# FFN inputs as 384 and 384 columns over two PSUM banks, gate with up in the last FFN, 64-row score products of two maps side by side

## The chip, the core and the metric

The kernel runs on one core of a Trainium2 chip. Its time is the time of one execution on the device in microseconds, the median of several runs. TensorE (PE in the rows) multiplies matrices and writes into PSUM; PEld is its weight load, which runs beside the matmuls. VectorE (DVE), ScalarE (ACT) and GpSimd (POOL) work on what it leaves. SyncE (SP) issues most transfers.

## The reference

Two layers over 512 latent tokens and 256 context tokens, 1024 channels wide, all in fp32. Each layer is a half FFN, a token mixer, and a second half FFN; each part is preceded by an RMS norm with shift and scale from a conditioning vector, and followed by another norm, a gate and the residual add. Layer 0 mixes by differential attention, layer 1 by a gated scan in both directions (HGRN2). In layer 1 the context tokens end with the mixer, so that the last FFN has only the 512 latent tokens.

```
def swiglu(h, w_in, w_out):
    gate, up = jnp.split(h @ w_in, 2, axis=-1)
    return (jax.nn.silu(gate) * up) @ w_out

# differential attention: 8 heads, two maps of 64 channels each
s = jnp.einsum('bqhmd,bkhmd->bhmqk', q, k) * scale
p = softmax(s)
a = p[:, :, 0] - lam * p[:, :, 1]

# HGRN2: q, two forget gates, input, output gate are projections of h
f = lb + (1 - lb) * sigmoid(f_logit)
```

The inner width of an FFN is 2816, so 22 chunks of 128 columns for the gate and 22 for the up part.

## The kernel before

Every fp32 operand of a large product is split in two: a high part (a cast on ScalarE) and a low part (the subtraction on VectorE), both of type fp32r. A product is then three passes, named in PASSES: high by high, high by low, low by high. `split` (lines 187 and 188) makes the two parts.

The order of all instructions is written by hand: each engine carries its instructions out in the order in which the program names them. The tile pools only add the waits: a new tile in a pool whose buffers are all in use waits until the last reader of an older tile is done.

**FFN.** `ffn` goes through the 22 chunks in groups, of which the first has one chunk and the seven others have three. For each chunk the gate is projected into a PSUM tile `pg`, the up part into `pu`, both from the pool ps_mm, which has two buffers of two banks (1024 columns) each. `proj` runs over the 8 slices of the contraction and the three passes, first for the 512 latent columns (24 matmuls into the first bank), then, where there is context, for the 256 context columns (24 matmuls into the second bank). ScalarE takes the silu of `pg`, VectorE multiplies it with `pu`, and the product is split into the tile `a`. After a group is complete, its output tiles (`out_tile`, line 653, 6 or 4 of them, each 18 matmuls of 512 columns which go to the two banks of a ps_mm tile in turn) are issued behind the gate of the next group's first chunk; VectorE adds each to `y` (line 670).

**Weights.** The class `Jobs` holds the list of all weight transfers and conversions in their order: gate, up and output weight of chunk 0, then of chunk 1, and so on. A transfer lands in one of three `raw` buffers, and is split into one of three `hl` buffers (gate and up) or three `wo` buffers. `need(key, ahead)` issues the conversions up to the one asked for and then up to `ahead` further gate or up weights; it stops at an output weight whose group is not open yet:

```
while self.done < n and self.gates.get(self.done, True) in self.open:
```

A group is opened by `J.open.add((l, i, c0))`, which stands behind the issue of the output tiles.

**Attention.** Heads are handled in four pairs; a generator `attn` is stepped by `T` between the matmuls of the next pair's projections (in the last pair: between those of the attention's output projection). An item is one head and 128 queries. For each of its two maps, `scores_softmax` multiplies a stacked operand of 128 rows (512 and 256 key columns) and then adds the missing product of 64 rows, with rows 0 to 63 for map 0 and 64 to 127 for map 1 (lines 954 and 955). VectorE takes the maximum of a map (line 957), then come the transposes of the item before, then the exponentials. The context queries have only the 256 context columns.

**HGRN.** For each of the 8 heads four projections of 128 channels go into tiles of the pool ps_tp (three buffers of one bank each): the two forget gates for all 768 columns, q and the output gate for 512. The sigmoids are lines 1388 (512 columns) and 1391 (256). Between the projections' matmuls `T` steps the scan of the head before.

## Time and profile before

| what | value |
|---|---|
| time, median of 3 runs | 3145.73 us (3143.97 to 3150.5) |
| the profiled execution's own time | 3149.13 us |
| its span, first to last instruction | 3147.3 us |
| TensorE busy | 3046.8 us, 97% |
| VectorE, ScalarE busy | 1716.1 and 961.3 us |
| mean granted TensorE clock | 0.985 |

The profile is that of one execution. Its span is 1.8 us shorter than that execution's time, and that time is 3.4 us above the median. A matmul's duration in the rows holds its way through the array, which overlaps with the next one; how fast matmuls follow each other is read from the starts, or from the length of a row that merges many.

### The profile page before, as it was taken

The numbers are of one execution on the slowest core, as the hardware profiler recorded it, in microseconds if no ns is written. First come the engines' busy times: TensorE is split into PE (matmuls) and PEld (weight loads), VectorE is DVE, ScalarE is ACT, GpSimd is POOL, SyncE is SP. The second block draws the span as 40 slices with busy tenths as digits, with TensorE's granted clock in tenths as the row PEclk, the third lists the DMA queues.
The fourth block names the chain that finished last, engine by engine and source line by source line (L and its number), as shares of the span: only waits on it lengthen the run. The fifth ranks groups of instructions, "written<-read, shape, count | busy, mean of one in ns | idle before, by whom it ended". The sixth has DMA issues, their size and how long they took to land.

```text
span 3147.3 us, 41132 instructions
## 1 busy us (share of the span) xinstructions
PE 3046.8 (97%) x17122; PEld 2577.1 (82%) x17122; DVE 1716.1 (55%) x2393; ACT 961.3 (31%) x1597; POOL 185.8 (6%) x235
## 2 busy tenths in 40 slices
PE   7999999989999899999999999999999999899998
PEld 5888888878877678888888888888889988678887
DVE  4555555646655674444446554444656565754344
ACT  4111111534444351111115111111444343442222
POOL 0000000131211020000001000000100000000000
PEclk9999999999988999999999999999999999999999
DMA  5333333254334233333222333333211111423231
GB/s 223 108 121 115 121 113 114 102 131 129 79 106 121 94 111 103 100 101 100 94 87 68 108 107 122 115 119 114 100 61 61 52 50 41 144 97 101 81 112 62
DMA packets 109546, 321.77 MB, mean 102 GB/s; under 512 B 11728, under 2 KB 12208, under 8 KB 109360
## 3 DMA queue, kind: packets, MB, share of 16 engines
q1 hardware_dynamic: 104432, 301.26, 30.4%
q0 software_dynamic: 3200, 11.59, 1.1%
q10 hardware_dynamic: 1728, 6.29, 0.5%
q8 instruction: 135, 2.21, 0.3%
q14 instruction: 51, 0.42, 0.0%
HBM read 292.83 MB, written 26.26 MB: 101 GB/s over the span
## 4 chain that ended last, share of the span: by engine, by line
PE 84%; DVE 4%; ACT 4%; issue 3%; DMA 2%; POOL 1%; SPq 0%; ACTq 0%; DVEq 0%; POOLq 0%
PE mm L574 43%; PE mm L653 21%; PE tp L574 8%; PE tp L1375 2%; PE mm L954 1%; PE gv L1012 1%; PE tp L653 1%; PE tp L1151 1%; PE mm L1285 1%; PE mm L955 1%; ACT tmp L395 1%; PE tp L992 1%; ACT tmp L545 1%; DMA mw<-in_w_mod_dram 1%; DVE hl L188 1%
## 5 line engine op out<-in xcount | busy, mean ns | idle before, releaser
L574 PE MATMUL mm<-hT,hl 128*128 128x256 f32 (+1 forms) x7728 | 1409.0, 342 | 8.1 <-DVE hT L550 3.3
L574 PEld LDWEIGHTS mm<-hT,hl 128*128 128x128 f32 x7728 | 1200.9, 188 | 208.1 <-DVE hT L550 6.7
L653 PE MATMUL mm<-wo,a 128*128 128x512 f32 x2886 | 664.9, 390 | 0.5 <-DVE wo L188 0.5
L653 PEld LDWEIGHTS mm<-wo,a 128*128 128x128 f32 x2886 | 538.5, 188 | 115.4 <-DVE y L668 2.6
L670 DVE TENSOR_TENSOR y<-y,mm 128x1024 f32<-128x1024 f32 x163 | 199.0, 1221 | 500.3 <-PE mm L653 500.3
L574 PE MATMUL tp<-hT,hl 128*128 128x512 f32 (+1 forms) x1824 | 381.4, 359 | 7.2 <-DVE aT L999 5.0
L188 DVE TENSOR_TENSOR hl<-raw,hl 128x1024 fp32r<-128x1024 f32 x250 | 304.6, 1229 | 149.8 <-ACT hl L187 149.8
L574 PEld LDWEIGHTS tp<-hT,hl 128*128 128x128 f32 x1824 | 291.4, 191 | 52.6 <-DVE aT L999 6.6
L292 DVE SCALAR_TENSOR_TENSOR acc<-mw,cs,acc 128x512 f32<-128x512 f32 x392 | 271.5, 745 | 2.8 <-DMA mw<-in_w_mod_dram 1.3
L187 ACT CAST a<-tmp 128x768 fp32r<-128x768 f32 (+1 forms) x88 | 68.8, 781 | 664.1 <-DVE tmp L747 664.1
L187 ACT CAST hl<-raw 128x1024 fp32r<-128x1024 f32 x250 | 258.2, 1046 | 25.3 <-DMA raw<-in_w_in_dram 20.6
L187 ACT CAST wo<-raw 128x1024 fp32r<-128x1024 f32 x94 | 98.0, 1044 | 464.0 <-PE mm L653 457.6
L731 ACT ACTIVATE tmp<-mm 128x768 f32<-128x768 f32 (+1 forms) x88 | 66.8, 759 | 405.4 <-PE mm L574 404.2
L747 DVE TENSOR_TENSOR tmp<-tmp,mm 128x768 f32<-128x768 f32 (+1 forms) x88 | 77.9, 886 | 200.8 <-PE mm L574 198.8
L188 DVE TENSOR_TENSOR a<-tmp,a 128x768 fp32r<-128x768 f32 (+1 forms) x88 | 78.5, 892 | 74.6 <-ACT a L187 74.6
L188 DVE TENSOR_TENSOR wo<-raw,wo 128x1024 fp32r<-128x1024 f32 x94 | 114.7, 1222 | 6.8 <-ACT wo L187 6.8
L653 PE MATMUL tp<-hl,hT 128*128 128x512 f32 x300 | 89.5, 432 | 16.5 <-DVE hl L188 5.1
L957 DVE TENSOR_REDUCE nm<-mm 128x1 f32<-128x768 f32 (+1 forms) x96 | 73.4, 776 | 54.8 <-PE mm L955 51.9
L653 PEld LDWEIGHTS tp<-hl,hT 128*128 128x128 f32 x300 | 55.7, 201 | 31.8 <-DVE aT L999 7.5
L964 ACT ACTIVATE pt<-mm,nm 128x768 f32<-128x768 f32 (+1 forms) x96 | 72.6, 767 | 29.5 <-DVE nm L957 29.4
L994 ACT CAST aT<-tp 128x384 fp32r<-128x384 f32 (+1 forms) x80 | 33.7, 461 | 144.5 <-PE tp L992 144.4
L1151 PE MATMUL tp<-hl,hT 128*128 128x256 f32 x576 | 75.1, 284 | 0.1
(189 smaller groups left out, 2439.0 us busy)
## 6 DMA issues: line engine op xcount, KB each, us to landing
raw<-in_w_in_dram SPq DMA_DIRECT2D x176, 512.0 KB, 4.5
mw<-in_w_mod_dram SPq DMA_DIRECT2D x144, 512.0 KB, 4.4
raw<-in_w_out_dram SPq DMA_DIRECT2D x88, 512.0 KB, 3.4
raw<-in_hg_w_dram SPq DMA_DIRECT2D x32, 512.0 KB, 3.3
raw<-in_da_qk_dram SPq DMA_DIRECT2D x16, 512.0 KB, 3.7
gg<-gg_d POOLq DMA_DIRECT2D x12, 512.0 KB, 4.6
xp<-x_d SPq DMA_DIRECT2D x10, 512.0 KB, 8.0
raw<-in_da_v_dram SPq DMA_DIRECT2D x8, 512.0 KB, 3.4
```

The costliest lines, as they stand in the source:

```text
L187: nc.scalar.copy(out=dst_hi, in_=src)
L188: nc.vector.tensor_tensor(out=dst_lo, in0=src, in1=dst_hi.bitcast(F32), op=ALU.subtract)
L292: nc.vector.scalar_tensor_tensor(out=acc[:, m], in0=raw[:, kk], scalar=cs[:, k, m:m + 1], in1=acc[:, m], op0=ALU.mult, op1=ALU.add)
L574: nc.tensor.matmul(out=ps_ap, lhsT=w[a], rhs=mv[b], start=(k == 0 and i == 0), stop=(k == nk - 1 and i == 2))
L653: nc.tensor.matmul(out=po if small else po[:, hh * 512:(hh + 1) * 512], lhsT=aT[ci][:, u, t * P:(t + 1) * P], rhs=wos[ci][:, v, hh * 512:( ...
L670: nc.vector.tensor_tensor(out=dst, in0=dst, in1=src, op=ALU.add)
L731: nc.scalar.activation(out=sg[:, :width], in_=pg[:, :width], func=AF.Silu)
L747: nc.vector.tensor_tensor(out=sg[:, :width], in0=sg[:, :width], in1=pu[:, :width], op=ALU.mult)
L957: nc.vector.tensor_reduce(out=nm, in_=sc[:, :n], axis=AX.X, op=ALU.max, negate=True)
L964: nc.scalar.activation(out=pt[:, :n], in_=scs[m][:, :n], func=AF.Exp, bias=nms[m], accum_out=s0s[hh][:, t:t + 1] if m == 0 else s1)
L1151: nc.tensor.matmul(out=pv[:, tt], lhsT=hT[:, k, a, t * P:(t + 1) * P], rhs=wk[:, b], start=(k == 0 and i_ == 0), stop=(k == KC - 1 and i_ ...
L1375: nc.tensor.matmul(out=pv[:, tt], lhsT=hT[:, k, a, t * P:(t + 1) * P], rhs=wk[:, b], start=(k == 0 and i_ == 0), stop=(k == KC - 1 and i_ ...
```

## The change

There are three edits.

1. A new helper `proj_banks` issues for each slice and pass one matmul for each of its blocks, each block with its own PSUM bank. In the three FFNs over 768 columns a projection now has two blocks of 384 columns, with the same weights, in the two banks of its ps_mm tile (`halves`); silu and multiplication read the two halves through a view (`flat`). The two forget gates of HGRN are done in the same way, in two ps_tp tiles, and each has two sigmoids of 384 columns.
2. In the last FFN (512 columns), from chunk 1 on, gate and up are issued together: one block each, the gate in the first bank of a single ps_mm tile and up in the second. Both calls of `need` stand in front of it, and so before `J.open.add`. The silu and the multiplication stay where they were.
3. In `scores_softmax` the 128-row products of both maps come first; then the 64-row products, for each block of key columns map 0 and map 1 one after the other. The two maximum reductions follow behind all of them.

```diff
--- before.py
+++ after.py
@@ -575,6 +575,16 @@
                 out=ps_ap, lhsT=w[a], rhs=mv[b],
                 start=(k == 0 and i == 0), stop=(k == nk - 1 and i == 2))
 
+    def proj_banks(blocks, tick=None):
+
+        for k in range(KC):
+            for i, (u, v) in enumerate(PASSES):
+                for w, ps, hT, a, b in blocks:
+                    nc.tensor.matmul(out=ps, lhsT=w[:, u, k], rhs=hT[:, k, v, a:b],
+                                     start=(k == 0 and i == 0), stop=(k == KC - 1 and i == 2))
+            if tick:
+                tick(3 * sum(e[4] - e[3] for e in blocks) / 2400.0)
+
     def proj(w, hT, pt, a, b, tick=None):
 
         for k in range(KC):
@@ -678,6 +688,15 @@
         pend = None
         hT = None
         slots = 2 * FC - 5
+
+        def halves(ap):
+
+            return ap.rearrange("p (b c) -> p b c", b=2)[:, :, 0:NTOK // 2]
+
+        def flat(ap, like):
+
+            return ap[:, :width].rearrange("p (b c) -> p b c", b=2) if len(like.shape) == 3 else ap[:, :width]
+
         J.open.add((l, i, 0))
         for gi, (c0, gn) in enumerate(GROUPS):
             aT = []
@@ -685,6 +704,8 @@
             for c in range(c0, c0 + gn):
                 pg = ps_mm([P, D])
                 pu = None
+                both = nt == LT and c != 0
+                pgv = pg[:, :width] if c == 0 or both else halves(pg)
                 if c == 0:
                     pu = ps_mm([P, D])
                     wg = J.need(("w", l, i, c, 0))
@@ -723,28 +744,33 @@
                     wg = J.need(("w", l, i, c, 0), 2)
                     M.pace(slots)
                     slots -= 1
-                    proj(wg, hT, pg[:, 0:NLAT], 0, NLAT)
-                    if nt == NT:
-                        proj(wg, hT, pg[:, NLAT:NTOK], NLAT, NTOK)
+                    if both:
+                        wu = J.need(("w", l, i, c, 1), 2)
+                        M.pace(slots)
+                        slots -= 1
+                        puv = pg[:, NLAT:2 * NLAT]
+                        proj_banks(((wg, pgv, hT, 0, NLAT), (wu, puv, hT, 0, NLAT)))
+                    else:
+                        proj_banks([(wg, pgv[:, b], hT, 384 * b, 384 * b + 384) for b in range(2)])
                 M.due()
                 sg = tmp([P, D])
-                nc.scalar.activation(out=sg[:, :width], in_=pg[:, :width], func=AF.Silu)
+                nc.scalar.activation(out=flat(sg, pgv), in_=pgv, func=AF.Silu)
                 if pend is not None:
                     aT_, wos_, first_ = pend
                     pend = None
                     for t in range(nt):
                         out_tile(t, aT_, wos_, y, first_)
                 J.open.add((l, i, c0))
-                if c != 0:
-                    pu = ps_mm([P, D])
+                if c == 0:
+                    puv = pu[:, :width]
+                elif not both:
+                    puv = halves(ps_mm([P, D]))
                     wu = J.need(("w", l, i, c, 1), 2)
                     M.pace(slots)
                     slots -= 1
-                    proj(wu, hT, pu[:, 0:NLAT], 0, NLAT)
-                    if nt == NT:
-                        proj(wu, hT, pu[:, NLAT:NTOK], NLAT, NTOK)
+                    proj_banks([(wu, puv[:, b], hT, 384 * b, 384 * b + 384) for b in range(2)])
                 M.due()
-                nc.vector.tensor_tensor(out=sg[:, :width], in0=sg[:, :width], in1=pu[:, :width], op=ALU.mult)
+                nc.vector.tensor_tensor(out=flat(sg, puv), in0=flat(sg, puv), in1=puv, op=ALU.mult)
                 a = fp.tile([P, 2, NTOK], F32R, tag="a", name="a", bufs=3)
                 split(a[:, 0, :width], a[:, 1, :width], sg[:, :width])
                 if c == FC - 2:
@@ -943,20 +969,23 @@
                 if t == 0:
                     s0s[hh] = sm.tile([P, NT], F32, tag="s0", name="s0", bufs=3)
                 s1 = sm.tile([P, 1], F32, tag="s1", name="s1")
-                nms, scs = [], []
+                nms = []
+                scs = [ps_mm([P, D]) for _ in range(2)]
+                cols = ([(slice(0, NLAT), slice(0, NLAT))] if t < LT else []) + [(slice(n - NCTX, n), slice(NLAT, NTOK))]
                 for m in range(2):
-                    sc = ps_mm([P, D])
-                    r0 = 64 * m
-                    for i in range(2):
-                        lhs = st_[:, m, t * P:(t + 1) * P] if i == 0 else st_[r0:r0 + 64, m, t * P:(t + 1) * P]
-                        rhs = st_[:, 2 + m] if i == 0 else st_[r0:r0 + 64, 4]
-                        if t < LT:
-                            nc.tensor.matmul(out=sc[:, 0:NLAT], lhsT=lhs, rhs=rhs[:, 0:NLAT], start=(i == 0), stop=(i == 1))
-                        nc.tensor.matmul(out=sc[:, n - NCTX:n], lhsT=lhs, rhs=rhs[:, NLAT:NTOK], start=(i == 0), stop=(i == 1))
+                    for o, i in cols:
+                        nc.tensor.matmul(out=scs[m][:, o], lhsT=st_[:, m, t * P:(t + 1) * P], rhs=st_[:, 2 + m, i],
+                                         start=True, stop=False)
+
+                for o, i in cols:
+                    for m in range(2):
+                        r = slice(64 * m, 64 * m + 64)
+                        nc.tensor.matmul(out=scs[m][:, o], lhsT=st_[r, m, t * P:(t + 1) * P], rhs=st_[r, 4, i],
+                                         start=False, stop=True)
+                for m in range(2):
                     nm = sm.tile([P, 1], F32, tag="nm", name="nm")
-                    nc.vector.tensor_reduce(out=nm, in_=sc[:, :n], axis=AX.X, op=ALU.max, negate=True)
+                    nc.vector.tensor_reduce(out=nm, in_=scs[m][:, :n], axis=AX.X, op=ALU.max, negate=True)
                     nms.append(nm)
-                    scs.append(sc)
                 lo = between()
                 pts = []
                 for m in range(2):
@@ -1383,17 +1412,18 @@
             for kd_ in range(4):
                 u = J.need(("hw", h, kd_), 2)
                 pl = ps_tp([P, 512])
-                proj(u, hT, pl, 0, NLAT, T)
                 if kd_ < 2:
-                    nc.scalar.activation(out=F[:, kd_, 0:NLAT], in_=pl, func=AF.Sigmoid)
-                    pc = ps_tp([P, 256])
-                    proj(u, hT, pc, NLAT, NTOK, T)
-                    nc.scalar.activation(out=F[:, kd_, NLAT:], in_=pc, func=AF.Sigmoid)
+
+                    pc = ps_tp([P, 512])
+                    proj_banks(((u, pl[:, 0:384], hT, 0, 384), (u, pc[:, 0:384], hT, 384, NTOK)), T)
+                    nc.scalar.activation(out=F[:, kd_, 0:384], in_=pl[:, 0:384], func=AF.Sigmoid)
+                    nc.scalar.activation(out=F[:, kd_, 384:], in_=pc[:, 0:384], func=AF.Sigmoid)
                     nc.vector.tensor_scalar(out=F[:, kd_], in0=F[:, kd_], scalar1=oml[:, kd_, h:h + 1],
                                             scalar2=lbv[:, kd_, h:h + 1], op0=ALU.mult, op1=ALU.add)
                     nc.vector.tensor_scalar(out=Kt[:, kd_], in0=F[:, kd_], scalar1=-1.0, scalar2=1.0,
                                             op0=ALU.mult, op1=ALU.add)
                 else:
+                    proj(u, hT, pl, 0, NLAT, T)
                     dst = qv if kd_ == 2 else gs
                     nc.scalar.activation(out=dst, in_=pl, func=AF.Sigmoid)
                     nc.vector.tensor_tensor(out=dst, in0=dst, in1=pl, op=ALU.mult)
```

## Rows read from the trace of the kernel before

**Rows 1.** The page: busy engines, and the chain by engine and line.
```profile
PE 3046.8 (97%) x17122; PEld 2577.1 (82%) x17122; DVE 1716.1 (55%) x2393; ACT 961.3 (31%) x1597; POOL 185.8 (6%) x235
...
PE 84%; DVE 4%; ACT 4%; issue 3%; DMA 2%; POOL 1%; SPq 0%; ACTq 0%; DVEq 0%; POOLq 0%
```

**Rows 2.** Stretches: length, busy PE PEld DVE ACT POOL (x count), PEclk, DMA share, GB/s.
```profile
640.00:990.00 350.00, 327.74 (x2005) 275.00 (x2004) 203.25 (x341) 148.11 (x332) 71.64 (x54) 0.95 0.45 117
...
2788.00:3122.00 334.00, 334.00 (x1443) 270.07 (x1442) 132.75 (x129) 82.97 (x101) 0.00 (x0) 1.00 0.29 92
```

**Rows 3.** Chain in order of time, first and last FFN: start, us, what.
```profile
359.59 24.50 PE mm L653 x108
384.09 8.40 PE mm L574 x48
...
2827.59 16.35 PE mm L653 x72
2843.93 33.60 PE mm L574 x144
```

**Rows 4.** Timeline of TensorE: attention-value product; last output tile.
```profile
762.60 2.31 PE L1012 MATMUL gv<-aT,vh 128*128 128x256 f32 x18
...
3134.64 4.24 PE L653 MATMUL tp<-wo,a 128*128 128x512 f32 x18
```

**Rows 5.** Timeline at a joint of two groups in the last FFN.
```profile
2842.20 1.99 ACT L187 CAST hl<-raw 128x1024 fp32r<-128x1024 f32 x2
...
2843.77 33.76 PE L574 MATMUL mm<-hT,hl 128*128 128x512 f32 x144
2843.97 1.22 DVE L670 TENSOR_TENSOR y<-y,mm 128x1024 f32<-128x1024 f32 x1 [2.87 <-PE mm L653]
2845.11 1.22 DVE L188 TENSOR_TENSOR wo<-raw,wo 128x1024 fp32r<-128x1024 f32 x1
...
2849.57 0.69 DVE L747 TENSOR_TENSOR tmp<-tmp,mm 128x512 f32<-128x512 f32 x1 [0.97 <-PE mm L574]
2850.29 0.62 ACT L187 CAST a<-tmp 128x512 fp32r<-128x512 f32 x1 [6.10 <-DVE tmp L747]
2850.82 1.04 ACT L187 CAST wo<-raw 128x1024 fp32r<-128x1024 f32 x1
...
2851.89 1.23 DVE L188 TENSOR_TENSOR wo<-raw,wo 128x1024 fp32r<-128x1024 f32 x1 [0.26 <-ACT wo L187]
```

**Rows 6.** Timeline of the first FFN's first output tiles.
```profile
70.14 2.59 DVE L668 COPY y<-mm 128x1024 f32<-128x1024 f32 x2 [3.56 <-PE mm L653]
...
71.42 2.59 PEld L653 LDWEIGHTS mm<-wo,a 128*128 128x128 f32 x12 [0.38 <-DVE y L668]
```

**Rows 7.** Busy time by stretch around two waits of TensorE, columns as in rows 2.
```profile
2755.00:2758.50 3.50, 0.00 (x0) 0.00 (x0) 2.63 (x3) 1.63 (x5) 2.41 (x4) 1.00 0.00 0
2758.50:2765.30 6.80, 5.82 (x24) 5.21 (x25) 3.96 (x7) 6.75 (x12) 2.60 (x4) 0.50 0.00 0
...
2461.50:2465.00 3.50, 3.50 (x19) 3.50 (x18) 1.98 (x3) 0.00 (x0) 0.24 (x1) 0.51 0.00 0
```

**Rows 8.** Timeline of one item's score products.
```profile
736.20 0.39 PE L954 MATMUL mm<-stk 128*128 128x512 f32 x1
...
736.43 0.28 PE L955 MATMUL mm<-stk 128*128 128x256 f32 x1
736.63 0.18 PEld L954 LDWEIGHTS mm<-stk 64*128 64x128 f32 x1 [0.24 <-issue]
...
736.97 0.28 PE L955 MATMUL mm<-stk 64*128 64x256 f32 x1
...
738.27 0.88 PE L992 MATMUL tp<-ident,pt 128*128 128x128 f32 x6
```

**Rows 9.** Timeline of TensorE: products with 32 output rows.
```profile
1199.01 0.64 PE L315 MATMUL gv<-acc,pick 128*32 128x128 f32 x16
```

**Rows 10.** The sigmoid of line 1388: ns min/median/max, first and last start, form.
```profile
L1388 ACT ACTIVATE F<-tp x16: 588/592/606, 2289.7 to 2651.6; 128x512 f32<-128x512 f32 x16
```

## The prediction

> **What bounds the kernel now.** I read the page's busy shares and its chain first [rows 1]. TensorE is busy 97% of the span and holds 84% of the chain; what is to be seen is that no other engine comes near, so a saving counts if it shortens the row of matmuls, and a loss counts if TensorE has to stand still. The stretches [rows 2] say where it stands: in the last FFN (2788 to 3122 us) it is busy 334.00 of 334.00 us, in the attention stretch 327.7 of 350. So the last FFN has no idle time that could soak up a new wait. The paces come from the chain in order of time [rows 3]: 48 matmuls of an FFN input (24 of 512 columns, 24 of 256) take 8.40 us; 144 of 512 columns in the last FFN take 33.60, so 233.3 ns each; 108 matmuls of the FFN output take 24.50, so 226.9 each. The 256-column ones are therefore (8.40 - 24 x 0.2333) / 24 = 116.7 ns. A pair of 512 and 256 costs 350 ns now.
>
> **Part 1, 384 and 384 columns over two banks.** The instruction count stays; 126 projections in the three long FFNs and 16 in HGRN, 24 pairs each, make 3408 pairs. No row has 384 columns. At 2.4 GHz 384 columns are 160 ns; the rows give what lies on top. On the same operands it is 10 ns at 256 columns and 20 ns at 512; the straight line gives 15, so 175 per matmul and 350 per pair: no change. The tempting reading is that the output's 227 comes from its two banks in turn. The trace speaks against that: the very last tile writes 9 matmuls in a row into one bank, and 18 of them take 4.24 us, of which the last one's own 0.39 comes off, so 3.85 / 17 = 226 ns [rows 4]. The attention-value product, also one bank, 256 columns, takes (2.31 - 0.28) / 17 = 119 ns, again some 13 on top. So 13 ns on top goes with other operands, not with alternation. If the pairs did get 13 ns: 346.7, or -3.3 x 3408 = -11 us. The ends: 10 on top gives 340 per pair, -34 us; 20 on top gives 360, +34 us. I take -3, next to the straight line on the same operands. In the last FFN 1008 matmuls could gain 6.4 ns each by the same argument (-6 us); I count nothing.
>
> **Part 2, gate with up in the last FFN.** Here the order of issue changes, and each engine works in that order. This is the joint of two groups today [rows 5]: TensorE goes from the last output tile to the up product at 2843.77 with no gap; three casts (the output weight, then gate and up weights of the next chunk) are issued before it, and ScalarE runs the last two from 2842.20; VectorE follows with the last add (2843.97), the three subtractions (the first at 2845.11) and only at 2849.57 the multiplication. All of it lies under the up product, 24 matmuls or 5.6 us. The new order takes this cover away at three places.
>
> (a) One PSUM buffer is held. Gate and up now fill one of the two ps_mm buffers, and its last reader, the multiplication, is issued behind the adds of the four output tiles. So the output tiles share the other buffer: each must wait for the add of the one before. Such a wait stands in the first FFN [rows 6]: a copy starts at 70.14 and TensorE resumes at 71.42, 1.28 later. The add starts 0.20 after TensorE would have gone on (2843.97 against 2843.77). One wait is 0.20 + 1.28 = 1.48 us; three per joint, seven joints: 31 us.
>
> (b) The next chunk's weights come late. At the first chunk of a group both J.need calls run before J.open.add, so they stop at the gated output weight. The casts that today run under the output tiles are issued only behind the multiplication and the split of a. Count from the instant TensorE could go on: add from 0.20, multiplication from 1.34 (VectorE's instructions start 1.14 apart, as 2843.97 and 2845.11), cast of a from 2.06 (0.72 after the multiplication's start), cast of the output weight from 2.59 (0.53 later), casts of gate and up from 3.54 and 4.49 (two casts take 1.99, one 1.04, so they start 0.95 apart). A subtraction starts 1.07 after its cast (2851.89 after 2850.82): that of the output weight at 3.66, behind it the gate's at 4.80 and the up's at 5.94, which ends at 7.17. The sixth matmul of the pair, up's low half, starts at 7.22; unhindered it would start at 5 x 0.233 = 1.17. 6.05 us, seven times: 42 us. Nothing else is queued on TensorE that it could do in that time.
>
> (c) Inside a group, need(up, 2) now asks for the up weight two units ahead, into the three hl buffers, while gate, up and the next gate hold all three. Its cast waits until the pair is done, then cast and subtraction take 1.07 + 1.23 = 2.30 us and end at 2.27, as the gate weight is free a little before the pair's end; sixth matmul at 2.32 instead of 1.17. 1.15 us for 13 chunk boundaries: 15 us. The silu and the multiplication queue behind these two on ScalarE and VectorE; their result is wanted only after the next pair, some 11 us later, so that costs nothing. The transfers run three ahead as before and have a whole pair of 11 us to land.
>
> Sum of (a) to (c): 88 us.
>
> (d) The clock. Before 2758.5 TensorE did nothing for 3.5 us and then stood at the lower level, 1.2 GHz, for 6.8 us; the 3.5 us from 2461.5 are at 0.51 with TensorE busy throughout, behind a shorter wait [rows 7]. (b) leaves TensorE idle for over 4 us seven times. The low stretch partly lies under the late weights; about 3.4 us of full work at half pace cost 1.7 us, seven times 12 us. The 34 short waits bring it on at times: if one in seven does, 8 us. I take 20; ends 0 and 55.
>
> **Part 3, the 64-row products.** For the two maps of one item TensorE needs, from 736.20 to 738.27, 2.07 us from the first product to the transposes [rows 8]. Where the height changes from 128 rows to 64 or back, the weight load starts only when the matmul before is nearly through (0.24 of idle, put down to issue), and the matmul behind it is 0.34 instead of 0.23 from its successor. Four such changes per item become two. With the 64-row products in turn: 0.23 + 0.12 + 0.23 + 0.20 + 0.34 + 0.23 + 0.12 + 0.20 = 1.67, a saving of 0.40; side by side, as the two halves use different rows and banks, 1.32, a saving of 0.75. If going from one half to the other cost as much as a change of height, 0.1 at best would be left. Over 32 items of 768 columns, and 16 of 256 at some 0.1 to 0.5: 5 to 32 us of TensorE, 24 if side by side works for the most part. The price: the first max reduction waits for both maps. Its result is wanted by the exponentials, the combination and the next item's transposes, an item (over 5 us) later, so most of it stays hidden; and 6% of that stretch is waiting already. I take -18; ends -30 and +5.
>
> The Trainium skill, TensorEngine Tiling (Array Packing), sections Key Properties and Theoretical Speedup, says that changing the tiling mode drains the engine, that tiles then work independently, and promises up to 2x for a contraction of 64. By it the whole 0.75 per item would come, 24 us from the 32 items; the trace agrees with the drain [rows 8], and for tiles at once it has only the products with 32 output rows, 16 of 128 columns in 0.64 us [rows 9].
>
> **Part 4, HGRN.** Both banks of a projection now end together, so the second forget gate's second half needs a tp buffer that the first gate's sigmoid has just begun to empty. The sigmoid on 512 columns takes 0.59 us [rows 10]; on 384 under that. TensorE reaches the place 0.4 us after its last start and waits to about 1.0: 0.5 us, 8 heads, 4 us; ends 0 and 8.
>
> **Sum.** The profiled execution took 3149.1 (span 3147.3); -3 + 88 + 20 - 18 + 4 gives 3240. The median of the runs is 3.4 lower, so I predict 3237.
>
> **The rivals.**
> The other side: the weights are there in time after all (the casts run ahead by some issue order or buffer that I read wrongly), and only the gains remain: 3149 - 3 - 18 + 4 - 3 = 3129. For it speaks that ScalarE is busy only 83 of 334 us there; against it that its queue is in order and the multiplication must pass first. It decides once the waits of part 2 stay under 17 us in all, or 2.4 per joint instead of some 13.
> Only the weights are late, and the output tiles keep two buffers: without (a), 3206. The buffer pool could hand on half a tile; against it, one tile is one allocation.
> The clock stays low: if each joint pulls the next two pairs, 22 us, down to half pace, 11 us each, 77 instead of 20: 3294. For it speaks the 0.50 [rows 7], against it that dense work follows.
> The pairs run at the bare column time, 320 ns: -30 x 3408 = -102, so 3138. It decides from 28 ns a pair. No row has a 512-column matmul below 226.
>
> **How the numbers follow.** The forecast has 0.74, one buffer wait less 0.10, the low clock 0.08, weights in time 0.06, bare columns 0.02. 3237 is the first. Its own range is 3195 to 3290, from the ends of the pair price (a third of them each way), the clock and the attention. It takes in the second rival and touches the third: 3195 to 3295. Within 0.2% (6 us, about what a measurement can tell here) is a chance meeting of gains and waits, 0.01; slower 0.92, faster 0.07.
>
> **What would show it.** In the last FFN the joint grows from 49.95 us (33.60 + 16.35) per group to about 63; TensorE's idle is put down to VectorE's adds (L670) between output tiles and to the hl subtraction at the first pair of a group; PE busy there falls under 90% and PEclk under 1. The long FFNs' 48 matmuls stay within 0.1 us of 8.40. The item from first score to transposes falls from 2.07 to 1.3 to 1.7. I am wrong if TensorE stays unbroken in the last FFN, or if 48 matmuls of 384 columns leave 8.15 to 8.64.

## The result and the profile after

The changed kernel takes 3234.56 us (median of 4 runs, 3233.65 to 3236.73) against 3144.85 for the kernel before beside it: ratio 1.0283, 95% interval 1.0266 to 1.0301. The forecast was 3237. The profiled execution took 3233.65 us, with a span of 3231.8.

Where the time went is read from the transposes ahead of each of the six parts (line 541 in both kernels), whose first start marks the boundaries:

| stretch, start to start | before, us | after, us | difference | forecast |
|---|---|---|---|---|
| three FFNs with context | 1741.0 | 1734.5 | -6.5 | -3 |
| attention | 513.3 | 492.1 | -21.2 | -18 |
| HGRN | 500.4 | 506.0 | +5.5 | +4 |
| last FFN and its end | 392.6 | 499.2 | +106.6 | +108 |

The table has one execution of each kernel, and its differences sum to 84.5 us where the medians differ by 89.7: the profiled execution of the kernel before took 4.3 us more than its median. So a difference of a few us is taken as shown only where a run below has it too.

First the page of the changed kernel: busy engines, the chain by engine, the costliest group and that of the output tiles.

```profile
PE 3037.8 (94%) x17122; PEld 2710.2 (84%) x17122; DVE 1711.0 (53%) x2393; ACT 961.0 (30%) x1597; POOL 185.3 (6%) x235
...
PE 81%; DVE 6%; ACT 5%; issue 3%; DMA 2%; POOL 1%; SPq 1%; ACTq 0%; DVEq 0%; POOLq 0%
...
L583 PE MATMUL mm<-hT,hl 128*128 128x384 f32 (+1 forms) x7056 | 1332.3, 349 | 45.7 <-ACT hl L187 43.4
...
L663 PE MATMUL mm<-wo,a 128*128 128x512 f32 x2886 | 671.0, 391 | 28.4 <-DVE y L680 23.6
```

Beside [rows 1], TensorE's share of the chain falls from 84% to 81% and the conversions' engines take it over. The idle time of these two groups has two owners by line: the casts of weights (43.4 us ahead of the projections, L583) and the adds of output tiles (23.6 us ahead of L663).

Next the stretch of the last FFN in the changed kernel, columns as in [rows 2]; then three stretches at one joint of two groups.

```profile
2788.00:3206.00 418.00, 355.64 (x1395) 269.36 (x1396) 125.35 (x122) 80.55 (x98) 0.00 (x0) 0.94 0.22 73
...
2914.70:2918.20 3.50, 0.06 (x1) 0.00 (x0) 2.51 (x3) 1.50 (x3) 0.00 (x0) 1.00 0.03 5
2918.20:2925.00 6.80, 5.58 (x12) 4.00 (x13) 4.67 (x4) 3.00 (x4) 0.00 (x0) 0.50 0.59 198
2925.00:2932.00 7.00, 7.00 (x31) 5.60 (x30) 1.28 (x2) 1.05 (x1) 0.00 (x0) 1.00 0.52 182
```

TensorE is busy for 85% of a stretch that it filled in [rows 2]. At each of the seven joints it stands still for over 4 us and then has one stretch of 6.8 us at 1.2 GHz; from one joint's stretch to the next the granted clock stays at 1.00.

The chain in order of time over one group (start, us, what) shows the whole price. It answers to 16.35 and 33.60 in [rows 3].

```profile
2893.59 4.12 PE mm L663 x18
...
2897.73 1.23 DVE y L680
...
2904.69 4.39 PE mm L663 x18
...
2910.39 4.39 PE mm L663 x18
...
2914.80 1.22 DVE y L680
2916.02 0.61 DVE tmp L773
...
2917.23 1.04 ACT wo L187
2918.27 1.90 ACT hl L187 x2
...
2920.21 13.20 PE mm L583 x46
...
2933.43 1.05 ACT hl L187
...
2934.51 1.24 DVE hl L188
...
2935.79 10.08 PE mm L583 x42
...
2948.30 10.30 PE mm L583 x43
2958.60 1.61 PE mm L663 x7
```

From 2893.59 to 2958.60 it is 65.0 us, against 49.95 before. Output tiles start 5.70 us apart (2904.69, 2910.39) where 18 x 0.227 = 4.09 is their work: the one buffer that is left. Behind the fourth tile follow the add, the multiplication, the casts of the output weight and of gate and up: the late weights. Pairs are counted here from the output tiles on: the first pair of a group is the one that starts behind them (chunk `c0 + 1` in the program), the third is the one ahead of the next output tiles. Ahead of the second and third pair stand a cast and a subtraction: all three hl buffers are full.

### The profile page after: what moved, and what is told of

Read it like the earlier page. It is cut to its first block, busy times and chain, and to the rows that moved or that the text cites. A ratio compares the mean times of both kernels' runs of the same rounds, so it can differ in the third digit from the quotient of the medians.

```text
span 3231.8 us, 41114 instructions
## 1 busy us (share of the span) xinstructions
PE 3037.8 (94%) x17122; PEld 2710.2 (84%) x17122; DVE 1711.0 (53%) x2393; ACT 961.0 (30%) x1597; POOL 185.3 (6%) x235
## 4 chain that ended last, share of the span: by engine, by line
PE 81%; DVE 6%; ACT 5%; issue 3%; DMA 2%; POOL 1%; SPq 1%; ACTq 0%; DVEq 0%; POOLq 0%
PE mm L583 40%; PE mm L663 20%; PE tp L574 5%; PE tp L583 3%; PE tp L1404 2%; PE mm L574 1%; ACT hl L187 1%; PE gv L1041 1%; PE tp L663 1%; DVE y L680 1%; DVE hl L188 1%; PE tp L1180 1%; PE mm L1314 1%; DVE nm L987 1%; ACT tmp L395 1%
## 5 line engine op out<-in xcount | busy, mean ns | idle before, releaser
L583 PE MATMUL mm<-hT,hl 128*128 128x384 f32 (+1 forms) x7056 | 1332.3, 349 | 45.7 <-ACT hl L187 43.4
L583 PEld LDWEIGHTS mm<-hT,hl 128*128 128x128 f32 x7056 | 1248.4, 189 | 120.3 <-ACT hl L187 55.9
L663 PE MATMUL mm<-wo,a 128*128 128x512 f32 x2886 | 671.0, 391 | 28.4 <-DVE y L680 23.6
L663 PEld LDWEIGHTS mm<-wo,a 128*128 128x128 f32 x2886 | 538.0, 188 | 151.2 <-DVE y L680 31.2
L574 PE MATMUL tp<-hT,hl 128*128 128x512 f32 (+1 forms) x1056 | 236.8, 372 | 12.0 <-DVE aT L1028 9.4
L574 PEld LDWEIGHTS tp<-hT,hl 128*128 128x128 f32 x1056 | 175.5, 194 | 43.7 <-DVE aT L1028 12.5
L583 PE MATMUL tp<-hT,hl 128*128 128x384 f32 x768 | 147.1, 342 | 6.7 <-ACT F L1419 6.7
L583 PEld LDWEIGHTS tp<-hT,hl 128*128 128x128 f32 x768 | 131.3, 188 | 8.7 <-ACT F L1419 8.6
L663 PE MATMUL tp<-hl,hT 128*128 128x512 f32 x300 | 88.0, 426 | 21.5 <-DVE aT L1028 9.7
L574 PE MATMUL mm<-hT,hl 128*128 128x256 f32 x672 | 97.2, 292 | 7.2 <-DVE hT L550 3.8
L574 PEld LDWEIGHTS mm<-hT,hl 128*128 128x128 f32 x672 | 84.6, 191 | 13.8 <-DVE hT L550 7.4
```

The lines of the kernel that those rows point to most:

```text
L574: nc.tensor.matmul(out=ps_ap, lhsT=w[a], rhs=mv[b], start=(k == 0 and i == 0), stop=(k == nk - 1 and i == 2))
L583: nc.tensor.matmul(out=ps, lhsT=w[:, u, k], rhs=hT[:, k, v, a:b], start=(k == 0 and i == 0), stop=(k == KC - 1 and i == 2))
L663: nc.tensor.matmul(out=po if small else po[:, hh * 512:(hh + 1) * 512], lhsT=aT[ci][:, u, t * P:(t + 1) * P], rhs=wos[ci][:, v, hh * 512:( ...
```

## The experiments

Each time is a median, and each ratio is to the kernel before, run beside it (3141.4 to 3144.9 us in the four sets of runs). The diffs are cuts, with `...` where lines are left out. They are against the changed kernel in the runs on the last FFN, against the kernel before in scores_only and ffn_only, and else against the run that the text varies.

### The three waits of the last FFN, one by one

**late_look: the chunk whose pair stands ahead of the output tiles (`c0`) asks for no further weight until they are issued.**

```diff
-                        wu = J.need(("w", l, i, c, 1), 2)
+                        wu = J.need(("w", l, i, c, 1), 0 if c == c0 else 2)
...
                 J.open.add((l, i, c0))
+                if both and c == c0:
+                    J.look(("w", l, i, c, 1), 2)
```

> The changed kernel, but at the first chunk of a group the look-ahead for the up weight comes after J.open.add, so that the three casts are issued ahead of the multiplication again. Theory of the prediction (waits in order of issue): the casts then run under the output tiles, but VectorE's add and three subtractions (1.22 and 1.14 apart) still stand between the last output tile and the up weight's low half: the sixth matmul of the pair at 4.9 us instead of 7.2, a wait of 3.7 instead of 6.05; 16 us less in all, and up to 14 more if the shorter idle time no longer brings the clock down: 3204 to 3219 us. Rival (the issue order behind J.open.add is the whole of it): the wait goes completely, 42 + 14 us less, 3178 us. Rival (the weights are not what the joint waits for): no change, 3235 us.

Measured 3221.74 us, ratio 1.024 (1.0193 to 1.0288): 13 us less, where the forecast said 15 to 31. A joint in its timeline:

```profile
2914.77 1.17 PE L583 MATMUL mm<-hT,hl 128*128 128x512 f32 x4 [1.41 <-DVE y L680]
...
2915.68 2.35 DVE L188 TENSOR_TENSOR hl<-raw,hl 128x1024 fp32r<-128x1024 f32 x2
...
2918.09 4.21 PE L583 MATMUL mm<-hT,hl 128*128 128x512 f32 x9 [0.34 <-DVE hl L188]
```

By the starts TensorE loses 1.57 us ahead of the first pair in place of 4.67, and what it waits for there is the last add, whose PSUM tile it needs. The subtractions of the output weight, of gate and of up stand behind that add on VectorE, as the expectation said: the pair's fifth and sixth matmul, the first to use the low halves, start 1.41 and 1.13 us behind the one before, the sixth at 2918.09, 4.88 us after TensorE could go on (2913.21), where 4.9 was expected. So the waits fell by the 16 us of the expectation. What did not come is the further gain from the clock: the low stretch stays at all seven joints, 3.4 or 6.8 us long. It now lies behind the sixth matmul, where no wait covers it: the matmuls of the last row start 0.43 us apart or more, where 0.23 is the full pace, and by the starts a joint loses some 2.0 us to it (an estimate), where warm, below, puts 1.5 on it in the changed kernel.

**small_tiles: the output tiles at the joint in halves, from the pool ps_tp.**

```diff
-                        out_tile(t, aT_, wos_, y, first_)
+                        out_tile(t, aT_, wos_, y, first_, small=both)
```

> The changed kernel, but the output tiles at the joints of the last FFN go half by half into the one-bank buffers of ps_tp instead of the ps_mm buffers. Theory: three waits of 1.48 us per joint go, seven joints, 31 us less: 3204 us; the waits on VectorE's adds vanish from TensorE's list. Rival (the output tiles had two buffers all along and the waits on the adds are those of the first group alone): no change, 3235 us.

Measured 3191.11, ratio 1.0143 (1.0098 to 1.0187): 43 us less, 12 more than the term. The waits between tiles are gone. A half tile's add is also shorter, and ends sooner behind the last matmul: the chain at the joint begins earlier, and at five of the seven joints the low stretch of the clock lasts 3.4 us in place of 6.8.

**fourth_hl: a fourth split weight buffer in the last FFN, paid for with the part of `xp` that only context tokens need.**

```diff
+        p, tag = (hlp, "hl") if quad[0] % 4 else (cur["hl4"], "hl4")
...
+        cur["hl4"] = st.enter_context(pool("hl4"))
-        xp = fp.tile([P, NT, D], F32, tag="x", name="xp")
+        xp = fp.tile([P, LT, D], F32, tag="x", name="xp")
```

> The changed kernel with a fourth buffer for the split gate and up weights in the last FFN. Theory: the cast of the up weight two units ahead need not wait for the pair, so 13 waits of 1.15 us go, 15 us less: 3220 us; the wait at the joint stays. Rival (the whole wait for casts is one of too few weight buffers): 15 + 42 us less, 3178 us.

Measured 3209.43, ratio 1.0201 (1.0152 to 1.0249): 25 us less against 15. The second and third pair of a group follow without a gap. The rest comes with the first pair of a group: the low stretch lasts 3.4 us at each joint.

**all_three: these three edits together.**

```diff
+                        wu = J.need(("w", l, i, c, 1), 0 if c == c0 else 2)
...
+                        out_tile(t, aT_, wos_, y, first_, small=both)
...
+    add_ffn(1, 1, conv_unit4)
```

> The three repairs together. Theory: what is left is the wait for VectorE at the joint (with the shorter adds some 3.1 us, seven times 22 us) over a kernel without edit 2, for which the sum of the other edits gives 3122 us: 3144 to 3156 us. Rival (gate with up gains by itself, as its matmuls change banks each time): 6 us lower, 3138. Rival (something else in the pair costs, such as two weights in turn): above 3165 us.

Measured 3161.05, ratio 1.0047 (1.0032 to 1.0063), between the expectation and the time from which its rival holds. Of the pair's price some 37 us are left (3161.05 less no_pair's 3124.28, below). Two neighbouring groups take 53.2 and 55.95 us. Three stretches at their joints, columns as in [rows 2]:

```profile
2890.00:2896.80 6.80, 4.58 (x17) 2.72 (x16) 5.10 (x6) 3.26 (x4) 0.00 (x0) 1.00 0.32 88
...
2943.50:2950.30 6.80, 4.57 (x15) 2.70 (x14) 4.80 (x6) 3.56 (x4) 0.00 (x0) 0.86 0.28 94
2950.30:2953.70 3.40, 3.40 (x10) 2.63 (x9) 2.02 (x3) 2.09 (x3) 0.00 (x0) 0.50 0.79 287
```

Two joints with the same work and the same 2.2 us of idle: behind one the clock stays at 1.00, behind the other it goes to 0.50. What is left is the joint's own conversions, which still wait for the output tiles, and at five of the seven joints the clock.

### The last FFN as it was

**no_pair: gate and then up again in the last FFN, the other parts of the change kept.**

```diff
-                both = nt == LT and c != 0
+                both = False
...
+                    if plain:
+                        proj(wu, hT, puv, 0, NLAT)
```

> The last FFN goes back to gate and then up, as in the kernel before; the 384 and 384 columns and the 64-row products stay. Theory (the whole loss sits in the last FFN; the other parts keep what the two traces show for them): the first FFNs -6.5, attention -21.3, HGRN +5.5, last FFN 0, so about 3122 us against 3144.9, ratio 0.993. Rival (part of the attention's gain is only given back later, or the last FFN loses for another reason than the pair): above 3135.

Measured 3124.28, ratio 0.9938 (0.9925 to 0.9951). The pair of gate and up costs about 110 us by itself, and the rest of the change is a gain. Its last FFN, by the chain in order of time:

```profile
2856.85 16.36 PE mm L663 x72
2873.21 33.60 PE mm L574 x144
```

That is the pace of [rows 3] again. The pair could not have gained on TensorE: its two 512-column matmuls over two banks follow each other 233 ns apart, as they do in one bank.

**warm: 19 matmuls that the result does not need, where TensorE stands idle.**

```diff
+                        if gi and c == c0 + 1:
+                            pd = ps_tp([P, 512])
+                            for _ in range(19):
+                                nc.tensor.matmul(out=pd, lhsT=hT[:, 0, 0, 0:P], rhs=hT[:, 0, 0, 0:NLAT], start=True, stop=True)
                         proj_banks(((wg, pgv, hT, 0, NLAT), (wu, puv, hT, 0, NLAT)))
```

> The changed kernel with 19 more matmuls of 512 columns (4.4 us, into a bank that nobody reads) ahead of the second pair of each group from the third group on, where TensorE stands idle for 4.5 us: seven times, 133 matmuls of work that the result does not need. Theory (the idle time brings TensorE down to 1.2 GHz for 6.8 us, which costs some 1.5 to 1.7 us where it lies under the late weights and up to 3.4 where it does not): the low stretches at the joints disappear and the time falls by 10 to 24 us, to 3211 to 3225. Rival (the low clock is hidden under the late weights): 3233 to 3237. Other rival (the added matmuls push the pair back): over 3240.

Measured 3223.23, ratio 1.0254 (1.0237 to 1.0271): 11 us less (10 in the last FFN's stretch of the two profiles), with 133 matmuls more. Two stretches at a joint of this kernel:

```profile
2912.40:2919.20 6.80, 6.16 (x26) 4.30 (x24) 5.50 (x6) 3.46 (x4) 0.00 (x0) 1.00 0.11 36
2919.20:2926.00 6.80, 6.34 (x28) 5.05 (x28) 2.96 (x3) 2.10 (x2) 0.00 (x0) 1.00 0.80 272
```

The clock stays at 1.00, and a group takes 63.5 us in place of 65.0. So the low clock is a cost of 1.5 us a joint, 10 to 11 in all: not hidden, but half of the forecast's 20. Most of the 6.8 us lies under the wait for the up weight's low half.

### The 64-row products

**scores_only: the kernel before with the 64-row products of both maps side by side.**

```diff
...
+                for o, i in cols:
+                    for m in range(2):
+                        r = slice(64 * m, 64 * m + 64)
+                        nc.tensor.matmul(out=scs[m][:, o], lhsT=st_[r, m, t * P:(t + 1) * P], rhs=st_[r, 4, i],
+                                         start=False, stop=True)
```

> The kernel before with the 64-row products of both maps side by side and nothing else. Theory (the 21 us between the two traces' attention stretches come from this edit alone): about 3123.5 us, ratio 0.993. Rival (part of the gain comes from the attention's neighbours, whose projections are also changed): above 3130.

Measured 3129.9, ratio 0.9953 (0.994 to 0.9966), so -10 to -19 us; the two profiled spans differ by 17.6, of which 17.0 lie in the attention stretch. Neither the theory's time nor the rival's is hit: this edit gives most of the 21 us. The medians differ by 12.7, less than the spans, as the profiled execution of the kernel before was a long one. The last few us come with the edit of the FFN columns around it: in ffn_only, below, the attention stretch is 2.8 us shorter without any change in it, in ffn_512_256_alt 5.2. How the one shortens the other is not shown. The stretch of the kernel before, with TensorE's waits in 640 to 1090 us of it (us in total, times, longest):

```profile
601.30:1114.60 513.30, 476.68 (x2802) 394.54 (x2800) 318.95 (x529) 227.71 (x485) 101.23 (x88) 0.95 0.40 112
...
PE tp L574 <- DVE aT L999: 5.0, 6, 2.8
PE tp L653 <- DVE aT L999: 5.0, 5, 2.3
...
PE tp L992 <- DVE pt L977: 3.4, 4, 1.2
```

And of scores_only (waits in 640 to 1074 us):

```profile
601.30:1097.60 496.30, 444.80 (x2802) 380.77 (x2800) 315.32 (x529) 227.76 (x485) 101.44 (x88) 0.95 0.41 116
...
PE tp L574 <- DVE aT L1002: 9.5, 9, 2.8
PE tp L995 <- DVE pt L980: 8.6, 8, 1.7
PE tp L653 <- DVE aT L1002: 8.1, 7, 3.1
```

TensorE's busy time falls by 31.9 us, yet the stretch only by 17.0: 14.9 us come back as idle time, behind VectorE's combination (pt) and copies (aT). An item of two maps takes 1.33 us from its first product to the transposes in place of 2.07, one of the context queries 0.64 in place of 1.14: 32 x 0.74 + 16 x 0.50 = 31.7.

**scores_apart: the same, with the 64-row products issued map by map.**

```diff
-                for o, i in cols:
-                    for m in range(2):
+                for m in range(2):
+                    for o, i in cols:
```

> The run of the 64-row products alone (3129.9 us), but with the four 64-row products map by map, so that a 512-column product is never followed by one on the other 64 rows: first map's 512 and 256 columns, then the second map's. Height changes stay at two an item. Theory (side by side is worth the part of 0.75 us an item that fewer changes do not give: 0.35 us over 32 items and some of it over 16): 8 to 12 us slower than that run, about 3139, an item from first score to transposes of about 1.67 us. Rival (only the number of height changes counts): 3130 within 3 us, item 1.3 to 1.4.

Measured 3130.8, ratio 0.9959 (0.9945 to 0.9973): the same as scores_only. But the rival is not shown by it. The query of line 957 from 736.24 to 736.30 in this kernel (ns min/median/max, first and last start, form):

```profile
L957 PE MATMUL mm<-stk x2: 493/494/495, 736.2 to 736.2; 64*128 64x512 f32 x2
```

Each map has one product of 512 columns in an item, and both start here 7 ns apart, although the program names the first map's product of 256 columns between them; the two of 256 columns follow together, 0.34 us later. So the halves work side by side with this order in the program too, and the run could not take the overlap away. The rows have starts alone: in what order the products stood in TensorE's queue they do not show.

### The columns

**ffn_only: 384 and 384 columns in the three long FFNs and nothing else.**

```diff
-                    proj(wg, hT, pg[:, 0:NLAT], 0, NLAT)
-                    if nt == NT:
-                        proj(wg, hT, pg[:, NLAT:NTOK], NLAT, NTOK)
...
+                        proj_banks([(wg, pgv[:, b], hT, 384 * b, 384 * b + 384) for b in range(2)])
```

> The kernel before with 384 and 384 columns over two banks in the three long FFNs and nothing else. Theory (173.3 ns where the pair is undisturbed, 176.7 in the stretches behind an interruption): -6.5 us, so about 3138, ratio 0.998. Had all 3024 pairs kept 346.7 ns against 350: -10. Rival (the 6.5 us come from elsewhere, the width changes nothing): 3143 to 3147.

Measured 3134.39, ratio 0.9975 (0.9965 to 0.9984): -5 to -11 us, as expected.

**ffn_384_in_turn: 24 matmuls into the first bank, then 24 into the second.**

```diff
-                        proj_banks([(wg, pgv[:, b], hT, 384 * b, 384 * b + 384) for b in range(2)])
+                        for b in range(2):
+                            proj_banks([(wg, pgv[:, b], hT, 384 * b, 384 * b + 384)])
```

> The run of the FFN columns alone (3134.4 us), but the 24 matmuls of the first 384 columns are issued before the 24 of the second, so a bank is written 24 times in a row and each weight half is loaded twice as far apart. Theory (the price follows from the columns and operands, not from going to and fro between banks): 48 matmuls in 8.32 to 8.40 us as before, 3134 within 4. Rival (the banks in turn are worth the difference between 13 and 15 to 20 ns on top): 48 matmuls in 8.5 or more, 3150 or above.

Measured 3133.92, ratio 0.9975 (0.996 to 0.999): the same.

**ffn_512_256_alt: 512 and 256 columns in the two banks in turn.**

```diff
-                        proj_banks([(wg, pgv[:, b], hT, 384 * b, 384 * b + 384) for b in range(2)])
+                        proj_banks([(wg, pg[:, 0:NLAT], hT, 0, NLAT), (wg, pg[:, NLAT:NTOK], hT, NLAT, NTOK)])
```

> The run of the FFN columns alone, but with 512 and 256 columns in the two banks in turn instead of 384 and 384: the order of the banks without the width. Theory (the pair costs 350 ns by its operands whatever the order): 48 matmuls in 8.40 us and about 3143 us, like the kernel before. Rival (the gain of that run comes from the order of the banks): 8.32 us, 3134.

Measured 3132.85, ratio 0.997 (0.996 to 0.9979): the same gain again, against my theory. The chains of the changed kernel, of ffn_384_in_turn and of ffn_512_256_alt, in that order:

```profile
357.37 24.53 PE mm L663 x108
381.90 8.32 PE mm L583 x48
```

```profile
255.22 8.33 PE mm L583 x48
```

```profile
255.54 8.32 PE mm L583 x48
```

All three orders take 8.32 to 8.33 us where [rows 3] has 8.40. In the last one the starts lie 228 ns apart behind a 512-column matmul and 118 behind one of 256. So 384 columns cost 173.3 ns (160 and 13) in one bank or in two, and 512 columns cost 228 on the very operands on which 512 behind 512 cost 233. The pair of gate and up has 512 behind 512 in two banks and shows 233. Neither the bank nor the operand decides alone, then: 512 columns directly behind 512 take 233 on the operands of the projections and 227 on those of the output [rows 3], also in one bank [rows 4]. Why stays open.

### The best of the parts

**ffn_scores: the FFN columns and the 64-row products; HGRN and the last FFN as before.**

```diff
+                proj(u, hT, pl, 0, NLAT, T)
...
-                    pc = ps_tp([P, 512])
-                    proj_banks(((u, pl[:, 0:384], hT, 0, 384), (u, pc[:, 0:384], hT, 384, NTOK)), T)
...
+                    pc = ps_tp([P, 256])
+                    proj(u, hT, pc, NLAT, NTOK, T)
```

> 384 and 384 columns in the three long FFNs alone, with the 64-row products; HGRN's projections and the last FFN as in the kernel before. Theory (HGRN's 5.5 us come from both halves of a projection ending together): 3144.9 - 6.5 - 21.3 = about 3117 us, 5 to 6 under the run that keeps HGRN changed. Rival (HGRN's loss comes from the 384-column pace or from what precedes it): same time as that run within 2 us.

Measured 3117.52, ratio 0.9915 (0.9902 to 0.9929). It is 6.8 us under no_pair, which differs in HGRN alone, and it is the fastest version that was run. In the changed kernel TensorE's waits of the HGRN stretch, which were led by other lines before, begin with the sigmoid:

```profile
PE tp L583 <- ACT F L1419: 6.7, 6, 1.8
```

In ffn_scores this wait is absent.

## Why the prediction was right, and where it was not

**What bounds the kernel.** Right: the last FFN had no idle time to soak up a wait, and lost as much time as TensorE stood still or ran at half clock there.

**(a) The held buffer.** Right in mechanism and size: 1.59 us a wait by the starts, 21 waits, 33 us against 31.

**(b) Late weights.** Right: the steps came out almost one by one. The cast of the output weight was put at 2.59 us and the gate's at 3.54 after TensorE could go on. The last matmul of the output tiles starts at 2914.37, so that instant is 2914.60, 0.23 later, and the pair's first start at 2919.27 is 4.67 behind it. The chain has the output weight's cast at 2917.23, 2.63 on, and the gate's begins at 2918.17, 3.57 on. The timeline of the joint:

```profile
2918.17 1.99 ACT L187 CAST hl<-raw 128x1024 fp32r<-128x1024 f32 x2
...
2919.27 0.79 PE L583 MATMUL mm<-hT,hl 128*128 128x512 f32 x1 [4.51 <-ACT hl L187]
2919.44 2.35 DVE L188 TENSOR_TENSOR hl<-raw,hl 128x1024 fp32r<-128x1024 f32 x2
...
2920.21 5.95 PE L583 MATMUL mm<-hT,hl 128*128 128x512 f32 x15 [0.15 <-ACT hl L187]
```

The up weight's subtraction ends at 2921.79, 7.19 on, against 7.17. One detail was other than said: TensorE waits already ahead of the gate's first matmul, so that the profile names the casts (43.4 us) and hardly the subtraction. By the starts it loses 4.67 us ahead of the pair and 1.07 ahead of its second and third matmul: 5.74 a joint against 6.05, 40 us against 42.

**(c) The three hl buffers.** 1.29 us at each of 13 places against 1.15: 17 us against 15. Most of it, 0.83 to 0.88 us, stands ahead of the pair's second matmul, for the cast, and only 0.2 ahead of the sixth. fourth_hl shows that it is the buffers.

**(d) The clock.** The sign was right and the term too large. All seven long idles brought the low clock, as forecast, and warm puts its price at 11 us (12 forecast for these). The 8 us for short waits were wrong: none of them brought it on. What (a) to (c) leave of the 106.6 us is some 16. Two of it are a wait that the forecast left out, ahead of the first joint. At the very first pair (chunk 1) the up weight's cast now stands behind the split of chunk 0's product, and the second matmul starts 2.32 us behind the first:

```profile
2760.20 0.51 PE L583 MATMUL mm<-hT,hl 128*128 128x512 f32 x1 [0.62 <-ACT tmp L757]
...
2761.42 1.04 ACT L187 CAST hl<-raw 128x1024 fp32r<-128x1024 f32 x1
...
2762.52 2.70 PE L583 MATMUL mm<-hT,hl 128*128 128x512 f32 x9 [1.81 <-ACT hl L187]
```

So some 3 us more than warm's 11 may be low clock under which another wait lay that warm laid bare; no run parts them.

**The pair price.** The term was -3, and it is -6.5 in the table and -8 in ffn_only, within its ends. The straight line through 256 and 512 columns was the step that failed: it gave 15 ns on top at 384 columns, and it is 13.3. The sentence that 13 ns go with other operands fell with it: ffn_512_256_alt has them on the same operands, as the mean of its two widths. That the two banks in turn are not what matters held.

**The scores.** -18 forecast, -17 by the spans of scores_only and -13 by its medians. Two errors nearly cancel: TensorE's saving was put at 24 with the halves side by side and is 31.9 (the 16 short items, put at 0.1 to 0.5, save 0.50 us each), and the price of the later maximum was taken as mostly hidden, which leaves 6 us, where 14.9 us of new waits stand. Whether these come from the later maximum or only from VectorE, which feeds a faster TensorE no faster, no run parts. The item itself, 1.32 forecast with the halves side by side, takes 1.33. The rows of one item in the changed kernel:

```profile
732.58 0.85 PE L977 MATMUL mm<-stk 128*128 128x512 f32 x4
733.37 0.62 PE L983 MATMUL mm<-stk 64*128 64x512 f32 x4
733.92 0.55 PE L1021 MATMUL tp<-ident,pt 128*128 128x128 f32 x3
```

In this item of the changed kernel the four 64-row products take 0.55 us from the first start to the transposes, where 512 and 256 columns twice in turn would be 0.35 longer by their paces. So about 0.39 of the 0.74 come from fewer changes of height and 0.35 from the overlap; that split is worked out from the rows and no run shows it. The Trainium skill, TensorEngine Tiling (Array Packing), section Key Properties, says that different tiles carry out weight loads and matmuls in parallel; the two starts 3 ns apart in this item agree.

**HGRN.** The place and the waiter were right, the size was not: waits of 1.1 us on average, where 0.5 was put down, 6 of them in place of 8.

Of the rivals, weights in time and a kept second buffer are excluded by the chain, a clock that stays low by the seven single stretches, and bare columns by 173.3 ns.

## What to carry to other kernels

When two accumulations share a buffer so that TensorE alternates between them, follow what the buffer's last reader is queued behind, and which conversions were issued under the matmuls that now come later: here the pair won nothing on TensorE, and three queues in order made over 90 us of waits out of it. Make the count joint by joint, in the order of issue of each engine; the starts of a handful of instructions in the old trace were enough to place the new ones 0.1 us from where they fell. Where TensorE is made faster, expect new waits for the engine that feeds it: here, in the attention stretch, with 6 to 7% of idle time, about half of the saving came back so.

## What was not expected of the hardware

- Two 64-row products on different row halves start within 7 ns of each other even when the program names a product of the first half between them (scores_apart). If TensorE's queue kept the program's order, the second half did not wait for its turn, and that each engine works strictly in that order does not hold for two row halves.
- On the operands of the projections 512 columns cost 233 ns directly behind 512 columns and 228 when 256 columns lie between; 384 columns cost 173.3 in both orders that were tried.
- Matmuls of 384 columns have a second pace, 176.7 ns: 144 of them take 25.16 us in most places and 25.64 in ffn_only from 179.72, behind an interruption by small products, where ffn_384_in_turn has 25.15 at the same place. What chooses the pace stays open.
- The same idle times are followed by the low clock at one joint and not at the next (all_three), and a low stretch lasts 3.4 or 6.8 us.
